# Projecting two column blocks with one 512-column product in a two-layer diffusion block

## The chip, the cores and the metric

The program runs on one core of a Trainium2 chip, in one launch. The metric is the device time of the whole program in microseconds, the median over the runs of a kernel. A profiled execution gives the trace; its times are counted from the first instruction of the span.

## What is computed

A two-layer backbone over 256 context and 512 latent tokens of width 1024. Each layer normalizes and modulates its input (`h`), projects it with one wide weight matrix, mixes tokens, gates, and projects back:

```
layer 0:  q, zf, zb, i, gate = split(h @ w_in, 5)      # each 2048 columns, 16 heads of 128
          o = bidirectional gated scan of (q, zf, zb, i), all 768 tokens
          y = rmsnorm(o) * norm_g * silu(gate);  x += gate_ada * (y @ w_out)
layer 1:  q, k, v, gate = split(h @ w_in, 4)           # each 2048 columns, 16 heads
          o = softmax(q1 k1) v - lam * softmax(q2 k2) v   (rotary q and k; 512 latent queries, 768 keys)
          y = rmsnorm(o) * g * silu(gate);  x += gate_ada * (y @ w_out)
final     rmsnorm(x)
```

So values (`i` in layer 0, `v` in layer 1) are wanted for all 768 tokens; the gate for all 768 in layer 0 and for the 512 latent ones in layer 1.

## The kernel before, in words

Every fp32 product of the projections is made of three products of split halves: a weight block is copied to `wH` (ACT, L269) and the remainder `wL = raw - wH` is made on DVE (L272); the input has `hH` and `hL`. A block of weights is a *unit* of 512 KB: it is loaded by SP's queue into one of four `raw` buffers (L261), split, and held in one of four `w` slots until TensorE (PE) has used it.

There are two kinds of projection. `proj_T` (L353) has the weights stationary and the tokens moving; it makes q, zf, zb of layer 0 and q, k of layer 1, one unit and one head at a time, with 256 and 512 moving columns. `proj_N` (L374) has 128 tokens stationary (`hH` or `hL`) and 256 weight columns moving; it makes the values and gates. One call is one token tile of 128: 8 blocks of the contraction times 3 products, 24 matmuls of 256 columns. `tok0` (layer 0) and `tok1` (layer 1) call it for a pair of heads: `tok0(p, "v")` and `tok0(p, "gate")` for six token tiles each, `tok1(p, "v1")` for six, `tok1(p, "sg")` for the four latent ones. There are eight pairs in each layer, so 8 x (6 + 6 + 6 + 4) x 24 = 4224 matmuls of this kind.

The order of all engines' instructions is written out by a planner, `Order`: processes (the scans or attention heads, the projections as one long process "fill", the loader, the two splits) yield priced operations, and the planner lists whichever can start first by its own prices; slots of buffers (`SLOTS`) are acquired and released on the way. `fill` takes the pieces in the order in which the end of the file lists them, and PE runs the scan's or the attention's short matmuls (L718, L740, L792, L807, L860, L889; L1403, L1404, L1433, L1442) between its steps. `out_proj` (L1066) projects back with 128 tokens of `y` stationary and 512 weight columns moving; the last `SLOTS["w"]` of its 16 blocks are taken together at the end, one token tile after the other (`rest`, L1100).

Two small jobs use `raw` directly, without a split: `ada_block` (L431; L445 on PE; four loads of 512 KB, half of the matmuls need the first two loads, half the last two) and `ada_gate`. Their units are put into the loader's list late: `piece` holds them back until at least `LATE` = 2 later units are listed (L308 to L322). In layer 0 the blocks `ada_block(1, b)` stand after zf of heads 10 to 13.

Of the kernel before, what the change touches and what calls it, by code (L numbers as in the profile page):

```python
# [35 lines left out]
RSQRT_SEED = 0x5F3759DF  # L36


SLOTS = {"bg": 2, "ps": 3, "pt": 1, "raw": 4, "raw0": 12, "w": 4, "y": 2, "q": 2, "FK": 2, "Q": 2, "t3": 3, "AD": 2,
         "A": 1, "S": 1, "KT": 2, "v": 2, "gate": 1, "hf": 2, "xgc": 2, "xnc": 2, "resc": 1, "jkc": 1, "hfc": 2,  # L40
         "Ks": 3, "S1": 3, "qL": 3, "rr": 2, "k": 1, "E": 2, "aT": 2, "v1": 2, "sg": 2}


# [157 lines left out]
def tile_kernel(ctx: ExitStack, tc: tile.TileContext, a: dict, out: bass.AP):  # L201
# [160 lines left out]
    def proj_N(acc, us, t, layer):  # L362

        n = KT * 3
        r = 1 if t < 2 else 0
        t0 = t - 2 + 2 * r
        sl = slice(t0 * P, (t0 + 1) * P)

        def step(kts):
            for kt in kts:  # L370
                un, k = us[kt // 4], kt % 4
                for j, (hh, W) in enumerate(((hH, un.H), (hH, un.L), (hL, un.H))):
                    i = 3 * kt + j
                    nc.tensor.matmul(acc, hh[r][:, kt, sl], W[:, k, :], start=(i == 0), stop=(i == n - 1))  # L374

        for kts in ((0, 1), (2, 3), (4, 5), (6, 7)):
            for kt in kts:
                yield wait(("h", layer, r, t0 // 2, kt))
            yield pe(6 * 0.109, lambda kts=kts: step(kts))


    start = ExitStack()
# [218 lines left out]
    def tok0(p, name, base):  # L601

        us = units_N(w0, base + p * 256)

        def evac(acc, ts):
            n = len(ts)
            pv = acc.rearrange("p (b c) -> p b c", c=256)[:, 0:n]
            dv = pairs[p][name][:, ts[0]:ts[0] + n]
            if name == "v":
                yield act(n * 256, lambda: nc.scalar.copy(out=dv, in_=pv))  # L610
            else:
                yield act(n * 256, lambda: nc.scalar.activation(out=dv, in_=pv, func=AF.Sigmoid))
                yield dve(n * 256, lambda: nc.vector.tensor_tensor(out=dv, in0=pv, in1=dv, op=ALU.mult))
            yield release("bg")
            if ts[0]:
                yield setev((name, p))

        def body():
            yield wait("scan")
            yield acquire(name)  # L620
            pairs[p][name] = env["sc"].tile([P, NT, 256], F32, name=name, tag=name, bufs=SLOTS[name])
            for ts in ((0, 1, 2, 3), (4, 5)):
                yield acquire("bg")
                acc = bg()
                for i, t in enumerate(ts):
                    yield from proj_N(acc[:, i * 256:i * 256 + 256], us, t, 0)
                yield spawn(evac(acc, ts), PR_EVAC)

        piece(us, body)

# [611 lines left out]
    def tok1(p, name, base):  # L1242
# [26 lines left out]

        piece(us, body)  # L1270

    def rope(acc, dst=None):

        at = env["ea"]
# [114 lines left out]
    def attention(n):  # L1389
# [99 lines left out]
            nc.vector.tensor_tensor(out=s["r"], in0=s["r"], in1=rs, op=ALU.mult)  # L1489

        def gated():
            s["y"] = env["at"].tile([P, 4, P], F32, name="y", tag="y1")
            for t in range(4):
                nc.vector.scalar_tensor_tensor(out=s["y"][:, t], in0=s["o"][:, t], scalar=s["r"][:, t:t + 1],
                                               in1=pair["sg"][:, t, cols], op0=ALU.mult, op1=ALU.mult)
# [4 lines left out]
                nc.tensor.transpose(s["pt"][:, t * P:(t + 1) * P], s["y"][:, t], ident)  # L1500

        def y_copy():
            yT = env["at"].tile([P, LAT], F32, name="yT", tag="y1")
# [148 lines left out]
    tok1(0, "v1", 2 * DI)  # L1652
    feat1_k(1)
    for n in range(NH):
        if n in (4, 5):
            piece(*ada_gate(1, n - 4, (0,)))
# [117 lines left out]
```

## Time and profile before

| | |
|---|---|
| runs | 1897.64, 1901.33, 1901.52 us; median 1901.33 us |
| the profiled execution | 1901.33 us, span of its instructions 1899.5 us |
| PE busy | 1858.8 us of the span (98%), 17910 matmuls |
| PE weight load / DVE / ACT busy | 1677.8 / 1250.5 / 932.6 us |
| mean DMA rate | 93 GB/s |

PE's busy time counts a matmul from its start until its result is out, and matmuls overlap; what a matmul costs in a stream is the distance from its start to the next one's start. The profiled execution is the median run, and its time is 1.8 us more than its span.

### The profile page before, as it was taken

Reading aid. Unit: us, or ns where it says so; the run is one execution under the profiler, and the core shown is the slowest. Engines: PE = TensorE matmul, PEld = TensorE weight load, DVE = VectorE, ACT = ScalarE, POOL = GpSimd, SP = SyncE. Lnnn points to the kernel's source line nnn. Section 1 sums busy time; section 2 is a strip of 40 time slices with the busy share of each in tenths; the row PEclk is TensorE's granted clock in tenths of the full one; section 3 lists DMA queues with packets and bytes.
Section 4 is the critical chain, followed back from the end, with each engine's and each line's share of the span. In section 5 each row is a group of like instructions: output and inputs, shape, how many; then the busy total and the mean of one; then the engine's idle time right before and its main releaser. Section 6 shows DMA issues by size and latency. Waiting matters only on the chain.

```text
span 1899.5 us, 41727 instructions
## 1 busy us (share of the span) xinstructions
PE 1858.8 (98%) x17910; PEld 1677.8 (88%) x17910; DVE 1250.5 (66%) x2492; ACT 932.6 (49%) x1716; POOL 29.9 (2%) x60
## 2 busy tenths in 40 slices
PE   5999999999999999999999899999999999999997
PEld 3898989999898998988988789999899999999986
DVE  4747657474664656657678776776667666766766
ACT  3434434343443434434455455665656565655753
POOL 0000000000000000000000100000000000000000
PEclk9999999999999999999999999999999999999999
DMA  9221121212313215131257751121322111121354
GB/s 312 60 68 52 44 75 44 64 36 73 101 33 116 72 54 159 50 109 46 66 168 259 227 163 45 33 68 51 110 86 73 42 60 51 51 73 67 104 201 172
DMA packets 166300, 177.59 MB, mean 93 GB/s; under 512 B 5857, under 2 KB 146066, under 8 KB 166114
## 3 DMA queue, kind: packets, MB, share of 16 engines
q1 hardware_dynamic: 160674, 156.08, 26.6%
q0 software_dynamic: 4864, 17.79, 2.7%
q8 instruction: 141, 2.31, 0.5%
q10 hardware_dynamic: 576, 1.05, 0.1%
q14 instruction: 45, 0.37, 0.1%
HBM read 161.52 MB, written 13.37 MB: 92 GB/s over the span
## 4 chain that ended last, share of the span: by engine, by line
PE 75%; issue 18%; DVE 3%; DMA 2%; ACT 1%; POOL 0%; SPq 0%; DVEq 0%; POOLq 0%; ACTq 0%
PE bg L353 21%; PE bg L374 15%; PE ps L353 7%; PE ps L374 7%; PE bg L1066 6%; PE ps L889 3%; PE ps L1442 3%; PE ps L740 2%; PE ps L860 2%; PE ps L1066 1%; PE bg L1403 1%; PE bg L1404 1%; PE pt L1433 1%; PE pt L840 1%; DVE wL L272 1%
## 5 line engine op out<-in xcount | busy, mean ns | idle before, releaser
L272 DVE TENSOR_TENSOR wL<-raw,wH 128x1024 fp32r<-128x1024 f32 x224 | 273.2, 1223 | 194.3 <-ACT wH L269 193.6
L269 ACT CAST wH<-raw 128x1024 fp32r<-128x1024 f32 x224 | 234.5, 1049 | 231.0 <-PE bg L353 88.4
L374 PE MATMUL bg<-wH,hH 128*128 128x256 f32 x768 | 226.8, 295 | 0.0
L374 PE MATMUL bg<-wH,hL 128*128 128x256 f32 x768 | 218.7, 285 | 0.0
L374 PE MATMUL bg<-wL,hH 128*128 128x256 f32 x768 | 218.2, 284 | 0.0
L353 PE MATMUL bg<-hH,wH 128*128 128x256 f32 x752 | 202.6, 350 | 1.4 <-ACT wH L269 1.2
L353 PE MATMUL bg<-hL,wH 128*128 128x256 f32 x752 | 194.0, 338 | 1.3 <-DVE hL L566 1.3
L353 PE MATMUL bg<-hH,wL 128*128 128x256 f32 x752 | 192.2, 337 | 0.0
L374 PE MATMUL ps<-wH,hH 128*128 128x256 f32 x640 | 186.4, 291 | 0.0
L374 PE MATMUL ps<-wL,hH 128*128 128x256 f32 x640 | 180.8, 282 | 0.0
L374 PE MATMUL ps<-wH,hL 128*128 128x256 f32 x640 | 180.7, 283 | 0.0
L1411 DVE TENSOR_REDUCE nm<-bg 128x1 f32<-128x768 f32 x128 | 118.9, 952 | 70.3 <-PE bg L1404 69.9
L353 PEld LDWEIGHTS bg<-hL,wH 128*128 128x128 f32 x752 | 141.3, 188 | 17.4 <-DVE hL L566 1.6
L353 PEld LDWEIGHTS bg<-hH,wL 128*128 128x128 f32 x752 | 141.2, 188 | 16.8 <-issue 0.2
L353 PEld LDWEIGHTS bg<-hH,wH 128*128 128x128 f32 x752 | 134.9, 189 | 19.7 <-issue 2.3
L374 PEld LDWEIGHTS bg<-wH,hH 128*128 128x128 f32 x768 | 146.9, 191 | 2.5
L353 PE MATMUL ps<-hH,wH 128*128 128x512 f32 (+1 forms) x400 | 147.2, 371 | 0.3 <-ACT hH L565 0.3
L374 PEld LDWEIGHTS bg<-wL,hH 128*128 128x128 f32 x768 | 147.0, 191 | 0.4
L1416 ACT ACTIVATE E<-bg,nm 128x768 f32<-128x768 f32 x128 | 115.6, 904 | 64.3 <-DVE nm L1411 62.7
L374 PEld LDWEIGHTS bg<-wH,hL 128*128 128x128 f32 x768 | 146.7, 191 | 0.3
L353 PE MATMUL ps<-hL,wH 128*128 128x512 f32 (+1 forms) x400 | 140.9, 355 | 0.1
L353 PE MATMUL ps<-hH,wL 128*128 128x512 f32 (+1 forms) x400 | 140.9, 355 | 0.0
(250 smaller groups left out, 3879.1 us busy)
## 6 DMA issues: line engine op xcount, KB each, us to landing
raw<-hg_w_in SPq DMA_DIRECT2D x80, 512.0 KB, 4.7
raw<-da_w_in SPq DMA_DIRECT2D x64, 512.0 KB, 4.1
raw<-w_ada SPq DMA_DIRECT2D x48, 512.0 KB, 4.3
raw<-hg_w_out SPq DMA_DIRECT2D x48, 512.0 KB, 4.4
raw<-da_w_out SPq DMA_DIRECT2D x32, 512.0 KB, 4.1
raw<-yT_d SPq DMA_DIRECT2D x15, 512.0 KB, 4.1
yT_d<-yT POOLq DMA_DIRECT2D x14, 384.0 KB, 4.2
yT_d<-yT POOLq DMA_DIRECT2D x14, 256.0 KB, 2.4
```

The costliest lines, as they stand in the source:

```text
L269: nc.scalar.copy(out=u.H, in_=u.raw)
L272: nc.vector.tensor_tensor(out=u.L, in0=u.raw, in1=u.H.bitcast(F32), op=ALU.subtract)
L353: nc.tensor.matmul(acc, W[:, kt, :], hh[r][:, kt, :], start=(i == 0), stop=(i == n - 1))
L374: nc.tensor.matmul(acc, hh[r][:, kt, sl], W[:, k, :], start=(i == 0), stop=(i == n - 1))
L740: nc.tensor.matmul(s["ps"][32 * b:32 * b + 32, (li + 1) % 2, c, :], s["C", li][:, o:o + 32], mv, start=True, stop=True, skip_group_check=T ...
L840: nc.tensor.transpose(s["pt"][:, i, d], st["K"][:, d, c * P:(c + 1) * P], ident)
L860: nc.tensor.matmul(s["sp"][:, i, d], s["KT", g][:, i, d], v[:, orders[d][k]], start=True, stop=True)
L889: nc.tensor.matmul(po[:, i], l, r, start=(k == 0), stop=(k == len(terms) - 1), skip_group_check=True)
L1066: nc.tensor.matmul(st["acc"][i][j], yy, W[:, 512 * j:512 * j + 512], start=(kt == 0 and k == 0), stop=(kt == NH - 1 and k == 2))
L1411: nc.vector.tensor_reduce(out=s["nm", qt][:, h:h + 1], in_=s["sc", qt, h][:, :, 0:384], axis=AX.XY, op=ALU.max, negate=True)
L1416: nc.scalar.activation(out=e, in_=s["sc", qt, h][:, :, 0:384], func=AF.Exp, bias=s["nm", qt][:, h:h + 1], accum_out=s["sums"][:, qt, h:h + 1])
L1442: nc.tensor.matmul(s["o"][:, qt], s["aT", qt][:, t], pair["v1"][:, t, cols], start=(t == 0), stop=(t == NT - 1), skip_group_check=True)
```

## The change

For seven of the eight pairs of each layer one piece takes the place of two: `both0` projects values and gate of a pair together, `both1` values and gate of layer 1. The moving operand is 512 columns, 256 of the values beside 256 of the gate, from units that hold 256 rows of the contraction and both column blocks; they are loaded with two DMAs each. A piece has four such units and needs all four for each token tile. The last pair of layer 0 and the first of layer 1 keep `tok0` and `tok1`. The value products of layer 1's two context tiles, which have no gate, stay 256 columns wide. The `w` slots become five, the `gate` slots two; `y` and `yT` of layer 1 share one buffer; the ada jobs move to other heads (`ada_gate` of layer 0 to after q of heads 4 and 6, `ada_block(1, b)` to after zf of heads 8, 10, 12, 14); the scratch for GpSimd's DMA descriptors is halved.

```diff
-SLOTS = {"bg": 2, "ps": 3, "pt": 1, "raw": 4, "raw0": 12, "w": 4, "y": 2, ...
-         "A": 1, "S": 1, "KT": 2, "v": 2, "gate": 1, "hf": 2, ...
+SLOTS = {"bg": 2, "ps": 3, "pt": 1, "raw": 4, "raw0": 12, "w": 5, "y": 2, ...
+         "A": 1, "S": 1, "KT": 2, "v": 2, "gate": 2, "hf": 2, ...
...
-        nc.sync.dma_start(out=u.raw, in_=u.src())
+        src = u.src()
+        if len(src.shape) < 4:
+            nc.sync.dma_start(out=u.raw, in_=src)
+        else:
+            for b in range(src.shape[2]):
+                nc.sync.dma_start(out=u.raw[:, :, b], in_=src[:, :, b])
...
+    def units_2(w, b, col):
+        return [Unit(lambda u=u: w[256 * u:256 * u + 256].rearrange("(k p) (b c) -> p k b c", p=P, c=DI)
+                     [:, :, b:b + 2, col:col + 256], [2, 2, 256], "w") for u in range(4)]
...
+    def proj_2(acc, us, t, layer, blocks=slice(0, 2)):
...
+        cost = 0.12 if blocks.stop == 1 else 0.23
+        def step(u):
+            for k in range(2):
+                kt, un = 2 * u + k, us[u]
+                for j, (hh, W) in enumerate(((hH, un.H), (hH, un.L), (hL, un.H))):
+                    i = 3 * kt + j
+                    nc.tensor.matmul(acc, hh[r][:, kt, sl], W[:, k, blocks].rearrange("p b c -> p (b c)"),
+                                     start=(i == 0), stop=(i == n - 1))
+        for u in range(4):
...
+            yield pe(6 * cost, lambda u=u: step(u))
...
+    def both0(p):
+        us = units_2(w0, 3, p * 256)
+        def evac(acc, t):
+            pv = acc.rearrange("p (t b c) -> p t b c", t=2, b=2)
+            v, g = (pairs[p][name][:, t:t + 2] for name in ("v", "gate"))
+            yield act(512, lambda: nc.scalar.copy(out=v, in_=pv[:, :, 0]))
+            yield act(512, lambda: nc.scalar.activation(out=g, in_=pv[:, :, 1], func=AF.Sigmoid))
+            yield dve(512, lambda: nc.vector.tensor_tensor(out=g, in0=pv[:, :, 1], in1=g, op=ALU.mult))
+            yield release("bg")
...
+            for t in range(0, NT, 2):
+                yield acquire("bg")
+                acc = bg()
+                for i in range(2):
+                    yield from proj_2(acc[:, i * 512:i * 512 + 512], us, t + i, 0)
+                yield spawn(evac(acc, t), PR_EVAC)
...
+    def both1(p):
+        us = units_2(w1, 2, p * 256)
...
+            if t < 2:
+                yield act(512, lambda: nc.scalar.copy(out=v[:, 0:2].rearrange("p t c -> p (t c)"), in_=acc))
+            else:
+                yield act(256, lambda: nc.scalar.copy(out=v[:, t], in_=acc[:, 0:256]))
+                yield act(256, lambda: nc.scalar.copy(out=g[:, t - 2], in_=acc[:, 256:512]))
+            yield release("ps")
...
-    tok0(0, "v", 3 * DI)
+    both0(0)
     for n in range(NH):
-        if n % 2 == 0 and n < NH - 2:
-            tok0(n // 2, "gate", 4 * DI)
         if n + 1 < NH:
             for i, (name, base) in enumerate(FEATS):
                 piece(*feat0(n + 1, unit_T(w0, base + (n + 1) * P), name))
-                if i == 0 and n in (7, 8):
-                    piece(*ada_gate(0, n - 7, (0, 1)))
-                if i == 1 and 9 <= n <= 12:
-                    piece(*ada_block(1, n - 9))
+                if i == 0 and n in (3, 5):
+                    piece(*ada_gate(0, (n - 3) // 2, (0, 1)))
+                if i == 1 and n in (7, 9, 11, 13):
+                    piece(*ada_block(1, (n - 7) // 2))
             if n % 2 and n < NH - 3:
-                tok0((n + 1) // 2, "v", 3 * DI)
+                both0((n + 1) // 2)
...
             feat1_k(n + 2)
             feat1_q(n + 2)
             if n % 2 == 0:
-                tok1((n + 2) // 2, "v1", 2 * DI)
-            else:
-                tok1((n + 1) // 2, "sg", 3 * DI)
+                both1((n + 2) // 2)
```

What the built programs show, at three places. On PE, the first token tile of the first pair of layer 0, from the last products of the head before; before:

```order
L353 MATMUL bg<-hL_82,wH 128x512
L353 MATMUL bg<-hH_81,wL 128x256
L353 MATMUL bg<-hH_80,wL 128x512
L374 MATMUL bg<-wH,hH_81 128x256
L374 MATMUL bg<-wL,hH_81 128x256
L374 MATMUL bg<-wH,hL_83 128x256
```

and now:

```order
L363 MATMUL bg<-hL_82,wH 128x512
L363 MATMUL bg<-hH_81,wL 128x256
L363 MATMUL bg<-hH_80,wL 128x512
L404 MATMUL bg<-wH,hH_81 128x512
L404 MATMUL bg<-wL,hH_81 128x512
L404 MATMUL bg<-wH,hL_83 128x512
```

One matmul stands where two stood. In the whole program 4224 of 256 columns become 1680 of 512 columns (L404), 336 of 256 columns for layer 1's context tiles (L404) and 528 that stay with `tok0` and `tok1` (L384); 17910 PE instruction records become 16230.

On PE, the first `ada_block(1, b)` of layer 0 (`raw` are its loaded weights, `sil` the stationary condition vectors); before, behind zf of head 10:

```order
L353 MATMUL bg_7158<-hH0_80,wL_6984 128x512
L740 MATMUL ps_7259<-Q_7141,C_7257 32x32 x24
L445 MATMUL ps_7308<-raw_7009,sil_100 32x128 x2
L445 MATMUL ps_7308<-raw_7051,sil_100 32x128 x2
...
L445 MATMUL ps_7308<-raw_7117,sil_100 32x128 x2
L445 MATMUL ps_7308<-raw_7209,sil_100 32x128 x2
```

and now, behind zf of head 8:

```order
L363 MATMUL bg_5246<-hH0_80,wL_4926 128x512
L476 MATMUL ps_5393<-raw_5134,sil_100 32x128 x2
L476 MATMUL ps_5393<-raw_5205,sil_100 32x128 x2
...
L800 MATMUL ps_5359<-Q_5229,C_5357 32x32 x24
L476 MATMUL ps_5393<-raw_5295,sil_100 32x128 x2
L363 MATMUL bg_5472<-hH1_81,wH_4968 128x256
...
L800 MATMUL ps_5476<-Q_5229,C_5444 32x32 x24
L363 MATMUL bg_5472<-hL0_82,wH_4968 128x512
L476 MATMUL ps_5393<-raw_5442,sil_100 32x128 x2
```

The fourth load's first product (`raw_5442`) now stands behind nine products of zb and two levels of the scan. On SP's queue the loads of that block, before and now, with what each waits for:

```order
L261 DMA raw_7009<-w_ada 128x4x256 [waits DMAHW5_49,DVE_49]
L261 DMA raw_7051<-w_ada 128x4x256 [waits DMAHW6_49,DVE_49]
L261 DMA raw_7117<-w_ada 128x4x256 [waits DMAHW7_49,DVE_49]
L261 DMA raw_7209<-w_ada 128x4x256 [waits DMAHW0_49,DVE_49]
```

```order
L263 DMA raw_5134<-w_ada 128x4x256 [waits DMAHW6_49,DMAHW5_49,DVE_49]
L263 DMA raw_5205<-w_ada 128x4x256 [waits DMAHW7_49,DMAHW0_49,DVE_49]
L263 DMA raw_5295<-w_ada 128x4x256 [waits DMAHW2_49,DMAHW1_49,DVE_49]
L263 DMA raw_5442<-w_ada 128x4x256 [waits DMAHW5_49,PE_49]
```

Before, all four loads wait for DVE, that is for a split that frees their buffer. Now the fourth waits for PE: its buffer is that of the first load, which the block's own first products read. The same stands at the blocks behind zf of heads 10 and 12; the one behind zf of head 14 has four loads that wait for DVE.

On PE, the finish of the last attention head in layer 1, from its last value products (`v` by `aT`) to the transposes of its result `y`; before (nine more rows of `out_proj` left out):

```order
L1066 MATMUL ps<-wH,yS_20245 128x512 x2
L1442 MATMUL ps<-v_19425,aT 128x128 x6
L1066 MATMUL bg<-wH,yKs 128x512 x2
...
L1066 MATMUL ps<-wL,hH_80 128x512 x2
L1066 MATMUL ps<-wH,hL_82 128x512 x2
L1066 MATMUL bg<-wH,yKs 128x512
L1500 MATMUL pt<-ident,y 128x128 x2
```

and now, all of them:

```order
L1547 MATMUL ps<-v_17852,aT 128x128 x6
L1126 MATMUL bg<-wL,yKs 128x512
L1126 MATMUL bg<-wH,yS_18693 128x512 x2
L1126 MATMUL bg<-wH,hH_80 128x512 x2
L1126 MATMUL bg<-wL,hH_80 128x512 x2
L1126 MATMUL bg<-wH,hL_82 128x512 x2
L1605 MATMUL pt<-ident,y 128x128 x4
```

Before, 25 products of `out_proj` stand between the two; now 9. The layer's last projections, which ran into the last head before, end while the head before it runs, and five blocks of `out_proj` instead of four are kept for the end.

At the program's start the order on ACT has one more split ahead of the first tokens: before, two `wH`, then `hH_80` and `hH_81` (the inputs of the first token tiles); now a third `wH` stands between `hH_80` and `hH_81`, since there is a fifth `w` slot.

## Rows read from the trace of the kernel before

**Rows 1.** The page: busy time, and PE's granted clock in 40 slices.

```profile
PE 1858.8 (98%) x17910; PEld 1677.8 (88%) x17910; DVE 1250.5 (66%) x2492; ACT 932.6 (49%) x1716; POOL 29.9 (2%) x60
...
PEclk9999999999999999999999999999999999999999
```

**Rows 2.** Windows: PE, PEld, DVE, ACT, POOL busy; clock; DMA share; GB/s.

```profile
0.00:60.00 60.00, 37.64 (x390) 27.36 (x390) 32.24 (x101) 22.90 (x39) 1.39 (x7) 1.00 0.84 266
...
240.00:352.00 112.00, 112.00 (x1428) 102.43 (x1427) 69.65 (x138) 46.16 (x88) 1.08 (x2) 1.00 0.18 55
...
1060.00:1110.00 50.00, 44.98 (x194) 35.55 (x193) 31.28 (x51) 20.93 (x28) 4.79 (x9) 0.97 0.72 218
...
1500.00:1600.00 100.00, 100.00 (x701) 94.55 (x700) 70.10 (x137) 60.36 (x118) 1.08 (x2) 1.00 0.18 56
...
1850.00:1900.00 50.00, 38.78 (x166) 30.72 (x164) 33.92 (x89) 19.49 (x29) 0.00 (x0) 0.94 0.47 164
```

**Rows 3.** Timeline of PE (start, us, engine, line), 256 columns moving, 96 products apart.

```profile
1433.24 0.28 PE L374 MATMUL ps<-wH,hH 128*128 128x256 f32 x1
...
1444.76 0.40 PE L353 MATMUL ps<-hH,wH 128*128 128x512 f32 x1
```

**Rows 4.** Timeline of PE, 512 columns: `out_proj`, 32 apart; `proj_T`, nine apart.

```profile
984.30 0.62 PE L1066 MATMUL bg<-wL,yF 128*128 128x512 f32 x2
...
991.73 0.63 PE L1066 MATMUL bg<-wH,yK 128*128 128x512 f32 x2
...
1448.95 0.39 PE L353 MATMUL ps<-hH,wH 128*128 128x512 f32 x1
...
1450.99 0.39 PE L353 MATMUL ps<-hH,wH 128*128 128x512 f32 x1
```

**Rows 5.** Groups by line and form on PE: values and gates.

```profile
L374 PE MATMUL bg<-wH,hH 128*128 128x256 f32 x768 | 226.8, 295 | 0.0
...
L374 PE MATMUL ps<-wH,hH 128*128 128x256 f32 x640 | 186.4, 291 | 0.0
```

**Rows 6.** Timeline of PE around the second `ada_block` of layer 1's parameters.

```profile
622.27 0.52 PE L353 MATMUL bg<-hL,wH 128*128 128x256 f32 x2
622.63 0.51 PE L353 MATMUL bg<-hH,wL 128*128 128x256 f32 x2
623.07 0.60 PE L740 MATMUL ps<-Q,C 128*32 128x32 f32 x46
...
623.52 1.93 PE L445 MATMUL ps<-raw,sil 128*32 128x128 f32 x62
625.38 0.61 PE L353 MATMUL bg<-hH,wH 128*128 128x256 f32 x2
```

**Rows 7.** The page, DMA issues: KB each and median us from issue to landing.

```profile
raw<-w_ada SPq DMA_DIRECT2D x48, 512.0 KB, 4.3
```

**Rows 8.** Timelines at the start: DVE, then PE's wait for it.

```profile
48.78 2.35 DVE L272 TENSOR_TENSOR wL<-raw,wH 128x1024 fp32r<-128x1024 f32 x2
...
51.79 0.49 PE L353 MATMUL bg<-hL,wH 128*128 128x512 f32 x1 [1.25 <-DVE hL L566]
```

**Rows 9.** Timeline of PE at the change of layers.

```profile
1080.79 0.89 PE L553 MATMUL ps<-ident,xn 128*128 128x128 f32 x4 [1.94 <-DVE hf L557]
...
1082.77 1.05 PE L1066 MATMUL bg<-wH,yK 128*128 128x512 f32 x2
1083.62 1.05 PE L1066 MATMUL bg<-wH,yF 128*128 128x512 f32 x2
```

**Rows 10.** Timeline of PE, the last head's last value products and transposes.

```profile
1828.53 1.50 PE L1442 MATMUL ps<-v,aT 128*128 128x128 f32 x12
...
1836.36 0.50 PE L1500 MATMUL pt<-ident,y 128*128 128x128 f32 x2 [0.54 <-DVE y L1494]
```

**Rows 11.** Waits: who waited for whom, us, times, longest.

```profile
DVE wL L272 <- ACT wH L269: 193.6, 103, 6.7
...
ACT wH L269 <- PE bg L353: 88.4, 19, 7.0
```

More of the change, by code (lines that the diff above doesn't have):

```diff
@@ L36 @@
 RSQRT_SEED = 0x5F3759DF
-SLOTS = {"bg": 2, "ps": 3, "pt": 1, "raw": 4, "raw0": 12, "w": 4, "y": 2, "q": 2, "FK": 2, "Q": 2, "t3": 3, "AD": 2,
-         "A": 1, "S": 1, "KT": 2, "v": 2, "gate": 1, "hf": 2, "xgc": 2, "xnc": 2, "resc": 1, "jkc": 1, "hfc": 2,
+SLOTS = {"bg": 2, "ps": 3, "pt": 1, "raw": 4, "raw0": 12, "w": 5, "y": 2, "q": 2, "FK": 2, "Q": 2, "t3": 3, "AD": 2,
+         "A": 1, "S": 1, "KT": 2, "v": 2, "gate": 2, "hf": 2, "xgc": 2, "xnc": 2, "resc": 1, "jkc": 1, "hfc": 2,
          "Ks": 3, "S1": 3, "qL": 3, "rr": 2, "k": 1, "E": 2, "aT": 2, "v1": 2, "sg": 2}
@@ L379, in proj_N @@
             yield pe(6 * 0.109, lambda kts=kts: step(kts))
+    def proj_2(acc, us, t, layer, blocks=slice(0, 2)):
+        n = KT * 3
+        r = 1 if t < 2 else 0
+        t0 = t - 2 + 2 * r
+        sl = slice(t0 * P, (t0 + 1) * P)
+        cost = 0.12 if blocks.stop == 1 else 0.23
[7 more added lines that the diff above has]
+        for u in range(4):
+            for kt in (2 * u, 2 * u + 1):
+                yield wait(("h", layer, r, t0 // 2, kt))
+            yield pe(6 * cost, lambda u=u: step(u))
     start = ExitStack()
@@ L627, in body @@
                 yield spawn(evac(acc, ts), PR_EVAC)
+        piece(us, body)
+    def both0(p):
[7 more added lines that the diff above has]
+            yield release("bg")
+            if t == NT - 2:
+                yield setev(("v", p))
+                yield setev(("gate", p))
+        def body():
+            yield wait("scan")
+            for name in ("v", "gate"):
+                yield acquire(name)
+                pairs[p][name] = env["sc"].tile([P, NT, 256], F32, name=name, tag=name, bufs=SLOTS[name])
+            for t in range(0, NT, 2):
[4 more added lines that the diff above has]
+                yield spawn(evac(acc, t), PR_EVAC)
         piece(us, body)
@@ L1270, in tok1, with tiles, evac, after @@
         piece(us, body)
+    def both1(p):
+        us = units_2(w1, 2, p * 256)
+        def tiles():
+            if "v1" not in apairs[p]:
+                apairs[p]["v1"] = env["at"].tile([P, NT, 256], F32, name="v1", tag="v1", bufs=SLOTS["v1"])
+                apairs[p]["sg"] = env["ea"].tile([P, NT - 2, 256], F32, name="sg", tag="sg", bufs=SLOTS["sg"])
+            return apairs[p]["v1"], apairs[p]["sg"]
+        def evac(acc, t):
+            yield wait("att")
+            v, g = tiles()
+            if t < 2:
[4 more added lines that the diff above has]
+            yield release("ps")
+            yield setev(("vg", p, t))
+        def after():
+            for t in (1, *range(2, NT)):
+                yield wait(("vg", p, t))
+            yield setev(("v1", p))
+            g = tiles()[1]
+            yield act(1024, lambda: nc.scalar.activation(out=g, in_=g, func=AF.Silu), extra=2.6)
+            yield setev(("sg", p))
+        def body():
+            yield acquire("v1")
+            yield acquire("sg")
+            for t in (*range(2, NT), 1):
+                yield acquire("ps")
+                acc = ps()
+                if t > 1:
+                    yield from proj_2(acc, us, t, 1)
+                else:
+                    for i in range(2):
+                        yield from proj_2(acc[:, 256 * i:256 * i + 256], us, i, 1, slice(0, 1))
+                yield spawn(evac(acc, t), PR_EVAC)
+            yield spawn(after(), PR_EVAC)
+        piece(us, body)
     def rope(acc, dst=None):
@@ L1491, in gated @@
         def gated():
-            s["y"] = env["at"].tile([P, 4, P], F32, name="y", tag="y1")
+            s["y"] = env["at"].tile([P, 4, P], F32, name="y", tag="y1", bufs=1)
             for t in range(4):
@@ L1502, in y_copy @@
         def y_copy():
-            yT = env["at"].tile([P, LAT], F32, name="yT", tag="y1")
+            yT = env["at"].tile([P, LAT], F32, name="yT", tag="y1", bufs=1)
             nc.scalar.activation(out=yT, in_=s["pt"], func=AF.Copy, scale=lc["gsub"])
@@ L1654, in tile_kernel @@
     for n in range(NH):
-        if n in (4, 5):
-            piece(*ada_gate(1, n - 4, (0,)))
+        if n in (4, 6):
+            piece(*ada_gate(1, (n - 4) // 2, (0,)))
         if n + 2 < NH:
@@ L1765 @@
     arrays.update(constants())
-    nc = _bacc.Bacc("TRN2", target_bir_lowering=False, num_devices=1, dynamic_dma_scratch_size=8192)
+    nc = _bacc.Bacc("TRN2", target_bir_lowering=False, num_devices=1, dynamic_dma_scratch_size=4096)
     aps = {n: nc.dram_tensor(n, v.shape, mybir.dt.from_np(v.dtype), kind="ExternalInput").ap()
```

## The prediction

> **What bounds the kernel now.** I read the page first. PE is busy for 1858.8 of 1899.5 us and its granted clock shows a 9 in all 40 slices [rows 1]. So PE is idle for 40.7 us, and no other engine comes near it: DVE is busy for 66% and ACT for 49%. The windows then say where that idle time lies [rows 2]: 22.4 us of it in the first 60 us, while the first weights and tokens come in, 5.0 us around the change of layers, 11.2 us in the last 50. In the two long stretches in which the values and gates are made, 240 to 352 us (layer 0) and 1500 to 1600 us (layer 1), PE is busy for the whole stretch at full clock (2.4 GHz), while DVE is busy for 69.65 of 112 us and 70.10 of 100, and ACT for 46.16 and 60.36. There only the price of PE's own instructions counts, and a new wait of PE is paid in full.
>
> A matmul's listed duration overlaps its neighbours, so I take distances between starts. 96 products of 256 columns take 1444.76 - 1433.24 = 11.52 us, or 120.0 ns each [rows 3]. 32 products of 512 columns in `out_proj` take 991.73 - 984.30 = 7.43 us, or 232.2 ns; nine in `proj_T` take 2.04 us, or 226.7 ns [rows 4]. So 512 columns cost a little less than twice 256.
>
> The sum is made against the profiled execution, 1901.33 us (its span and 1.8 us around it), which is also the median of the three runs.
>
> **Merged products (gain).** The groups of [rows 5] and their sisters hold 3 x 768 + 3 x 640 = 4224 products of 256 columns. The orders count 1680 pairs of them that become one of 512. A pair costs 2 x 120.0 = 240.0 ns. No row has a 512-column product with exactly these operands; the nearest is `out_proj`, which also has tokens stationary and split weights moving, 232.2 ns, and the fastest is `proj_T`, 226.7 ns. The gain per pair is 7.8 to 13.3 ns, or 13.1 to 22.3 us for 1680. I take 231 ns, close to the first, since its operands are the same in kind: 9.0 ns x 1680 = **-15.1 us**.
>
> The Trainium skill, page "TensorE: Matmul & The Clock Gate", section "Back-to-back issue gap", gives a stream's start-to-start time at full clock as N/2.4 + about 2.5 ns. By it, a merged pair saves one 2.5 ns, and the sum of this term, as an estimate from that page, would be -4.2 us. The rows do not bear that out: they show 120.0 and 227 to 232 ns where it has 109 and 216.
>
> **The moved ada blocks (loss).** These are small products of the condition vectors with `w_ada`, which need no split. Before, the four loads of an `ada_block` wait for splits on DVE and are in time: PE runs the block's 64 passes without a wait, from 623.52 to 625.38 [rows 6]. Now the fourth load of three blocks (behind zf of heads 8, 10 and 12) waits until PE has finished with the block's first buffer. From its issue to its landing such a load takes 4.3 us [rows 7]. PE's work in between, by the order: four more products of the block (0.06 us each, 1.86 / 32), two levels of the scan (623.07 to 623.52, 0.45 us each), ten products of zb, 256 and 512 columns in turn (0.36 us a pair, 622.27 to 622.63: 1.8 us): 0.24 + 0.9 + 1.8 = 2.9, some 3.0 us. The rest, 1.3 us, is a wait of PE, and behind it stands all of PE's stream, the next level of the scan too. Three times: **+3.9 us**. The ends are my choice around that median, since no row shows a disturbed load here: 3.2 us a load leaves 0.2 each, 0.6 in all; half as long again, 6.5 us, leaves 3.5 each, 11 in all.
>
> **The start (loss).** PE waits 1.25 us for `hL`, which DVE makes behind two `wL` of 2.35 us together [rows 8]. A third split now stands ahead of it on ACT and on DVE. One `wL` costs 1.2 us, and what it delays is that wait: between 0 (if DVE is free meanwhile) and 1.2; I take **+1.0 us**. The first pair now needs gate weights early, too. It begins 20 us later, so I price it at nothing; its cover is the last head-0 projection.
>
> **The last head (loss).** Before, the last value products end at 1828.53 + 1.50 = 1830.03 and the transposes of `y` begin at 1836.36: 6.3 us for squares, the reciprocal root and the gating on ACT and DVE [rows 10]. PE filled these with 25 products of `out_proj` and waited 0.54 us. Now 9 products stand there, 9 x 0.232 = 2.1 us, so the wait becomes 6.3 - 2.1 = 4.2, or 3.7 us more. The 16 products come later, where nothing needs cover, so this is lost. The chain may be shorter with fewer splits in between, or the scores before it may wait too: 0.5 to 8; I take **+3.8 us**.
>
> **At nothing.** Evacuations become 256 and 512 columns in other shapes, but ACT and DVE have 40 to 60 us to spare in 100 or so [rows 2]. Loads become two DMAs, 56 more issues on SP; at the DMA share of 0.18 in those windows the queue has room. The piece holds four of five `w` slots for some 33 us; the next unit's cast and `wL` must fit beside the one projection that is prefetched, 24 pairs of 0.35 us = 8.3 us, and they take 1.2 us each. If that cover is missing, see the slower rival. One buffer for `y` and `yT`: heads are some 40 us apart. The smaller scratch has no row; I take 0, bounds 0 to 2.
>
> **Sum:** -15.1 + 3.9 + 1.0 + 3.8 = -6.4, so about **1895 us**. With the small ends of the losses and the middle of the gain it is 1887; with the large ones 1906.
>
> **Rivals.** *(a) The gain without the losses.* The loads of the ada blocks come earlier than the order suggests, or the last chain is shorter. Then only the merging counts, -13 to -22 us: about 1885. For it: PE is 100% busy in the stretches at stake. Against it: the two waits follow from the order itself, not from a price.
>
> *(b) The gain is eaten.* The ada waits are at their large end, 11 instead of 3.9 us: 1895 + 7.1 = 1902. A clock loss can join it: behind the wait of 1.94 us at the change of layers, two pairs of 512-column products start 0.85 us apart, 425 ns a product [rows 9], the lower of the clock's two levels (1.2 GHz). Four such products behind each of three waits are 12 x (425 - 232) = 2.3 us more: 1904. For it: those idle times of 1.9 us are as short as a long ada wait. Against it: the median load, and a granted clock of 0.97 over the whole change of layers [rows 2].
>
> *(c) Slower: the pieces wait for splits.* A piece frees four slots within one token tile, and the splits of the next units queue on ACT behind evacuations. DVE's mean wait for a `wH` is 193.6 / 103 = 1.9 us, the longest 6.7 [rows 11]. If PE waits that long at the end of each of the 14 pieces, it is +26.6 us: 1895 + 26.6 = 1921.5. It decides from 6.4 / 14 = 0.46 us a piece. Against it: the 8.3 us of cover.
>
> *(d) The columns alone set the price.* Then 512 columns cost what 2 x 256 do, 240.0 ns, the gain is 0 and the losses remain: 1901.3 + 8.7 = 1910. For it: the two distances of [rows 3] and [rows 4] are nearly in the ratio of the columns. Against it: both rows of [rows 4] lie below 240. The page named above has nearly this rule, as it leaves 2.5 ns a pair.
>
> That the change does not do what it says is out: the orders count 1680 merged products and 16230 records on PE.
>
> **How the numbers follow.** My forecast has a chance of 0.50, with a range of its own from 1889 to 1900; rival (a) 0.22, (b) 0.17, (c) 0.06, (d) 0.05. The range goes from 1881, which takes in the middle of (a) and most of its gain, to 1905, which takes in (b). A measurement of this kernel tells 0.2% (3.8 us) from no change. Faster than 1897.5 are (a) and five sixths of the forecast: 0.22 + 0.42 = 0.64. Within 3.8 us are the rest of the forecast (0.08), (b) without its tail (0.14) and a little of (a) and (d): 0.25. Slower are (c), most of (d) and the tail of (b): 0.11.
>
> **What the profile after would show.** If the gain is right: starts of L404's 512-column products 230 to 232 ns apart, PE's busy time some 15 us less, in both long windows alike. If the ada step is right: waits of about 1.3 us on PE for the fourth load of three of the four blocks. If the end is right: a wait of some 4 us ahead of the last transposes of `y`, ended by DVE's `y`. Wrong would be: 237 ns or more a product, no wait at the ada blocks, or new idle time of PE behind each piece.

## The result, and the profile after

| | before | after |
|---|---|---|
| runs | 1897.64 to 1901.52 us | 1911.41 to 1917.63 us |
| median | 1901.30 us | 1913.24 us |
| ratio | | 1.0067 (95%: 1.0055 to 1.0079) |
| profiled execution's span | 1899.5 us | 1910.6 us |

The change made the kernel 12 us slower. The forecast was 1895 us, and the range ended at 1905. The page of the changed kernel, its lines on busy time and on the clock (to be read beside [rows 1]):

```profile
PE 1852.3 (97%) x16230; PEld 1586.8 (83%) x16230; DVE 1249.6 (65%) x2499; ACT 933.8 (49%) x1758; POOL 30.2 (2%) x60
...
PEclk9999999999999999999999899999999999999999
```

PE's busy time fell by 6.5 us, not by 15, and its idle time rose from 40.7 to 1910.6 - 1852.3 = 58.3 us, by 17.6. Most of it stands in PE's waits after (who waited for whom: us in all, times, longest):

```profile
PE ps L476 <- DMA raw<-w_ada: 13.7, 5, 9.9
PE pt L1605 <- DVE y L1599: 10.5, 7, 6.6
PE ps L584 <- DVE hf L588: 10.0, 3, 8.1
...
PE ps L800 <- DVE AD L804: 1.1, 2, 0.7
...
PE ps L1126 <- ACT hH L1613: 0.8, 1, 0.8
PE ps L920 <- ACT KT L904: 0.6, 1, 0.6
```

and before:

```profile
PE ps L445 <- DMA raw<-w_ada: 12.3, 3, 10.7
PE ps L553 <- DVE hf L557: 4.9, 2, 2.9
...
PE pt L1500 <- DVE y L1494: 0.5, 1, 0.5
...
PE ps L740 <- DVE AD L744: 0.3, 1, 0.3
```

Two waits grew by 15.1 us together: for `y` at the transposes of a head's result, 0.5 to 10.5, and for `hf`, the input of layer 1, 4.9 to 10.0. The waits for `w_ada` grew by 1.4 in all and by 2.2 behind the start. The merged products themselves are cheap, as the timeline of PE at the first piece shows:

```profile
72.96 0.40 PE L404 MATMUL bg<-wH,hH 128*128 128x512 f32 x1
...
79.78 0.39 PE L404 MATMUL bg<-wH,hH 128*128 128x512 f32 x1
```

The second row is the 30th product after the first: 6.82 us / 30 = 227.3 ns, against 240.0 for the two that it replaces [rows 3]. (Over layer 0's undisturbed products, those between two of their own kind, the distances lie between 220 and 250 ns, 229 on average, in the same trace, whose starts come in steps of 10 ns.) So the gain was there, and something took back more than it gave. The windows around the change of layers and at the end add a second loss, the granted clock (the column after the five engines; before [rows 2]):

```profile
1060.00:1110.00 50.00, 41.88 (x180) 33.52 (x179) 29.01 (x49) 19.26 (x26) 3.94 (x8) 0.90 0.68 204
1110.00:1200.00 90.00, 88.64 (x586) 81.91 (x585) 68.97 (x120) 50.90 (x88) 0.00 (x0) 0.98 0.25 74
...
1850.00:1911.00 61.00, 50.06 (x208) 40.09 (x208) 42.58 (x105) 24.59 (x37) 0.00 (x0) 0.92 0.40 137
```

0.90 around the change of layers where it was 0.97, and 0.92 in the end part where it was 0.94. Behind the longest wait of the end part, products of 512 columns run at the lower level of the clock, as they did behind the shorter waits of before [rows 9]; the timeline of PE there:

```profile
1850.47 1.16 PE L1605 MATMUL pt<-ident,y 128*128 128x128 f32 x4 [6.64 <-DVE y L1599]
1852.40 1.22 PE L1126 MATMUL ps<-wH,hH 128*128 128x512 f32 x2 [0.78 <-ACT hH L1613]
1853.42 1.05 PE L1126 MATMUL ps<-wL,hH 128*128 128x512 f32 x2
1854.28 1.05 PE L1126 MATMUL ps<-wH,hL 128*128 128x512 f32 x2
```

The last two start 0.86 us apart, a pair of products in each row, where 0.46 is usual.

**The wait for `hf`.** It ends the chain DMA, ACT, DVE, PE. One row of each, from their timelines after:

```profile
1036.73 14.22 SPq L263 DMA_DIRECT2D raw<-hg_w_out  x4
...
1060.97 0.38 SPq L263 DMA_DIRECT2D raw<-yT_d  x1
```

```profile
1074.11 1.04 ACT L274 CAST yF<-raw 128x1024 fp32r<-128x1024 f32 x1 [8.32 <-DMA raw<-yT_d]
```

```profile
1075.19 1.23 DVE L277 TENSOR_TENSOR yK<-raw,yF 128x1024 fp32r<-128x1024 f32 x1 [6.03 <-ACT yF L274]
```

```profile
1079.51 0.69 PE L584 MATMUL ps<-ident,xn 128*128 128x128 f32 x2 [8.12 <-DVE hf L588]
```

DVE runs its operations in the order listed. It stands 6.03 us at the split of a block of `y` whose load was issued at 1060.97 and was there at about 1074, 13 us later, and `hf` is queued behind that split. Two groups of loads ahead of it on SP's queue, four loads of `hg_w_out` were drawn out over 14.22 us, as they waited for buffers. This gave the first theory: **the kept blocks.** With five `w` slots, `out_proj` keeps five blocks for the end of each pair of token tiles (L1160 after), uses them for one token tile after the other and frees them only with the second, and the loads stand still meanwhile. The second: **the late heads.** The piece puts a pair's gates ahead of the next head's k and q. Each odd head then starts later against the projections, and the last head outlives them. A third: **the long steps.** The planner hands out six 512-column products at a time (1.37 us instead of 0.72), and the heads' short products wait longer.

### The profile page after: what moved, and what is told of

The parts are those of the page before. It is cut to its first block, busy times and chain, and to the rows that moved or that the text cites. A ratio compares the mean times of both kernels' runs of the same rounds, so it can differ in the third digit from the quotient of the medians.

```text
span 1910.6 us, 38544 instructions
## 1 busy us (share of the span) xinstructions
PE 1852.3 (97%) x16230; PEld 1586.8 (83%) x16230; DVE 1249.6 (65%) x2499; ACT 933.8 (49%) x1758; POOL 30.2 (2%) x60
## 4 chain that ended last, share of the span: by engine, by line
PE 71%; issue 20%; DVE 4%; DMA 3%; ACT 2%; POOL 0%; SPq 0%; DVEq 0%; POOLq 0%; ACTq 0%
PE bg L363 20%; PE bg L404 13%; PE bg L1126 6%; PE ps L404 6%; PE ps L363 5%; PE ps L949 3%; PE ps L1547 2%; PE ps L800 2%; PE ps L920 2%; PE bg L384 2%; PE ps L1126 2%; PE bg L1508 1%; DVE wL L277 1%; PE pt L1538 1%; PE bg L1509 1%
## 5 line engine op out<-in xcount | busy, mean ns | idle before, releaser
L404 PE MATMUL bg<-wH,hH 128*128 128x512 f32 x336 | 138.0, 411 | 0.0
L404 PE MATMUL bg<-wL,hH 128*128 128x512 f32 x336 | 131.7, 392 | 0.0
L404 PE MATMUL bg<-wH,hL 128*128 128x512 f32 x336 | 131.6, 392 | 0.0
L404 PE MATMUL ps<-wH,hH 128*128 128x512 f32 (+1 forms) x336 | 123.9, 369 | 0.0
L789 ACT COPY C<-K 128x768 f32<-128x768 f32 x80 | 74.4, 930 | 98.7 <-DVE K L814 83.7
L404 PE MATMUL ps<-wH,hL 128*128 128x512 f32 (+1 forms) x336 | 120.0, 357 | 0.0
L404 PE MATMUL ps<-wL,hH 128*128 128x512 f32 (+1 forms) x336 | 119.1, 355 | 0.0
L1543 ACT COPY aT<-pt 128x512 f32<-128x512 f32 (+1 forms) x128 | 61.3, 479 | 100.6 <-PE pt L1538 100.3
L1547 PEld LDWEIGHTS ps<-v,aT 128*128 128x128 f32 x768 | 95.2, 191 | 4.0
```

The source lines that it names most:

```text
L404: nc.tensor.matmul(acc, hh[r][:, kt, sl], W[:, k, blocks].rearrange("p b c -> p (b c)"), start=(i == 0), stop=(i == n - 1))
L789: nc.scalar.copy(out=C.rearrange("p (n d s) -> p n d s", d=2, s=z), in_=view(st["K"], 0, [[2 * z, TOK // (2 * z)], [TOK + z, 2], [1, z]]))
L1543: nc.scalar.copy(out=s["aT", qt][:, lo:hi].rearrange("p a b -> p (a b)"), in_=s["pt"][:, 0:(hi - lo) * P])
L1547: nc.tensor.matmul(s["o"][:, qt], s["aT", qt][:, t], pair["v1"][:, t, cols], start=(t == 0), stop=(t == NT - 1), skip_group_check=True)
```

## Experiments

**1. Four kept blocks, five slots.**

```diff
-            if kt >= NH - SLOTS["w"]:
+            if kt >= NH - 4:
```

> The changed kernel with four instead of five blocks kept for the end of each out_proj; five w slots stay. Theory of the kept blocks (the fifth w slot makes out_proj keep five blocks, so loads stand still while these are used, and the waits at the change of layers, 9.8 us for hf, and at the last head, 6.6 us for y, follow from that): the wait for hf falls to about 5 us as before, the time falls by 4 to 8 us, to 1905 to 1909. Theory of the late heads (the one long piece puts the gates ahead of the next head's k and q, so the last head ends late and outlives the projections): the wait for y stays at 5 to 8 us, the time changes by less than 3 us.

Measured: 1900.34 us, ratio to before 0.9999 (0.9988 to 1.0010): 12.9 us less than the changed kernel, more than either theory gave. Its waits of PE:

```profile
PE pt L1605 <- DVE y L1599: 10.3, 7, 5.8
PE ps L584 <- DVE hf L588: 3.7, 2, 3.5
```

The wait for `hf` fell (10.0 to 3.7, below the 4.9 of before), the wait for `y` stayed. So the kept blocks explain the change of layers, and not the last head. The four loads that took 14.22 us now take 7.67, on SP's timeline; the kernel before, then this one:

```profile
1042.01 6.80 SPq L261 DMA_DIRECT2D raw<-hg_w_out  x4
```

```profile
1036.94 7.67 SPq L263 DMA_DIRECT2D raw<-hg_w_out  x4
```

What holds them up in the changed kernel stands on ACT, in the cast of a block of `y`; the kernel before, the changed one, and this one:

```profile
1044.76 1.05 ACT L269 CAST yF<-raw 128x1024 fp32r<-128x1024 f32 x1 [1.24 <-PE bg L1066]
```

```profile
1047.84 1.05 ACT L274 CAST yF<-raw 128x1024 fp32r<-128x1024 f32 x1 [6.80 <-PE bg L1126]
```

```profile
1041.95 1.05 ACT L274 CAST yF<-raw 128x1024 fp32r<-128x1024 f32 x1 [1.23 <-PE bg L1126]
```

Blocks 8 to 11 of `out_proj` (of 0 to 15) read one of the two buffers for `y`, which is given back when block 11 has been used for the second token tile. With blocks 12 to 15 kept, that comes ahead of the end part. With five kept, block 11 is one of them, and the next `y` waits until PE is through with all five for the first token tile and with block 11 for the second. Its cast stands ahead of the next weights' casts in ACT's order, so the buffers that the loads want stay taken: SP waits 7.9 us for the split of this `y`. That it is this buffer, more than the slots of the weights, is read from the code and these rows, not tried by itself.

The granted clock from 1060 to 1110 us is 0.97 again. The profiled execution took 1905.61 us, the longest of this kernel's ten runs; its span of 1903.8 us is 6.8 less than that of the changed kernel.

**2. The fifth slot alone, in the kernel before.**

```diff
-"raw0": 12, "w": 4,
+"raw0": 12, "w": 5,
...
-name="y", tag="y1")
+name="y", tag="y1", bufs=1)
...
-name="yT", tag="y1")
+name="yT", tag="y1", bufs=1)
...
-dynamic_dma_scratch_size=8192
+dynamic_dma_scratch_size=4096
```

> The kernel before with the fifth w slot alone (and the smaller buffers that make room for it: one buffer for y and yT, the halved scratch); all projections as before, 256 columns. Theory of the kept blocks: 5 to 10 us slower than before, 1906 to 1911, with waits for hf of 8 to 10 us and for y of 3 us or more. Theory of the late heads: within 2 us of before, 1899 to 1903, a wait for y below 1 us.

Measured: 1908.33 us, ratio 1.0042 (1.0028 to 1.0056), 7.6 us slower than before without one merged product. PE's wait for `hf`, and the draw-out of the four loads on SP's timeline:

```profile
PE ps L553 <- DVE hf L557: 9.6, 3, 7.8
```

```profile
1044.79 14.22 SPq L261 DMA_DIRECT2D raw<-hg_w_out  x4
```

PE has no row of waiting for `y` at all. (In ACT's order the cast of `y` waits 6.80 us for PE here too.) The theory of the kept blocks holds for the change of layers, and its guess about the last head was wrong.

**3. The same with four kept blocks** (experiment 2 with the edit of experiment 1).

> Against e2_w5 (1908.3 us): the kernel before with the fifth w slot (and the smaller buffers) and four blocks kept for the end of out_proj; no merged products. Theory of the kept blocks: the wait for hf falls from 9.6 us to about 5, the time by 5 to 8 us, to that of the kernel before within 2 us (1899 to 1903). Rival (the fifth slot costs by itself, in the order of loads and splits): 1905 or more.

Measured: 1902.05 us, ratio 1.0004 (0.9995 to 1.0013); the wait for `hf` is 4.2 us in all. The fifth slot, the smaller buffers and the halved scratch cost nothing that can be measured; keeping five blocks does, 6.3 us here. (The two kernels of experiment 6 also differ by this alone: 8.0 us.)

**4. The last pair of layer 1 separate** (in the changed kernel: `tok1` for its values, then k and q of head 15, then `tok1` for its gates).

```diff
-            if n % 2 == 0:
+            if n % 2 == 0 and n < NH - 4:
                 both1((n + 2) // 2)
+            elif n == NH - 4:
+                tok1(NH // 2 - 1, "v1", 2 * DI)
+            elif n == NH - 3:
+                tok1(NH // 2 - 1, "sg", 3 * DI)
```

> The changed kernel with the last pair of layer 1 separate again: its values before k and q of head 15, its gates after them. Theory of the late heads: head 15 starts some 10 us earlier against the end of the projections, the wait for y at the last head falls from 6.6 us to 0 to 3, the time by 3 to 7 us, to 1906 to 1910, although 96 pairs of products (about 1 us) are no longer merged. Theory of the kept blocks: the wait for y stays near 6 us, and the time is 0 to 2 us longer, 1913 to 1915.

Measured: 1910.00 us, ratio 1.0045 (1.0030 to 1.0060), 3.2 us less than the changed kernel, though the two intervals overlap; and the wait at the last head stayed, 6.35 us. The time went the way of the theory and its reason did not. The timeline of PE says why:

```profile
1763.33 0.40 PE L363 MATMUL ps<-hH,wL 128*128 128x512 f32 x1
...
1783.34 0.34 PE L1509 MATMUL bg<-Ks,qL 128*128 128x384 f32 x1
1789.07 0.42 PE L1508 MATMUL bg<-Ks,S 128*128 128x384 f32 x1
```

q of head 15 is complete at 1763.33, but its first score starts only at 1789.07, as head 14's last one came at 1783.34. Head 14 was late; by the order, head 13 was late ahead of it, as its k and q still stood behind a piece. One pair was not enough to try the theory.

**5. Two pairs separate, and four kept blocks** (heads 12 to 15; experiment 1 and, for both pairs, the edit of experiment 4).

> Against e1_rest4 (1900.3 us): four blocks kept, and the last two pairs of layer 1 (heads 12 to 15) separate, their gates after the next head's k and q. In its order 24 products of out_proj stand between the last value products and the transposes of y, where e1_rest4 has 4. Theory of the late heads: the wait for y at the last head (5.8 us in e1_rest4) falls below 1 us, the time by 3 to 6 us, to 1894 to 1897, less about 2 us that 192 pairs no longer merge. Rival (the chain of the last head itself is longer in this program, whatever the order of the pieces): a wait of 4 us or more stays, the time is that of e1_rest4 or up to 2 us more.

Measured: 1895.82 us, ratio 0.9974 (0.9964 to 0.9984), 4.5 us under experiment 1, although 192 pairs of products are no longer merged. Timelines of PE, the last product of q of head 15 and its first score, and later the last value products and the transposes of `y`; the kernel after first, then this one:

```profile
1782.30 0.40 PE L363 MATMUL ps<-hH,wL 128*128 128x512 f32 x1
...
1796.34 0.42 PE L1508 MATMUL bg<-Ks,S 128*128 128x384 f32 x1
```

```profile
1756.80 0.40 PE L363 MATMUL ps<-hH,wL 128*128 128x512 f32 x1
...
1769.65 0.34 PE L1508 MATMUL bg<-Ks,S 128*128 128x384 f32 x1
...
1776.58 0.28 PE L384 MATMUL ps<-wH,hL 128*128 128x256 f32 x1
...
1824.60 1.50 PE L1547 MATMUL ps<-v,aT 128*128 128x128 f32 x12
...
1832.23 1.01 PE L1605 MATMUL pt<-ident,y 128*128 128x128 f32 x4 [0.59 <-DVE y L1599]
```

After the change, q of head 15 was the last projection of all, and the head's first score came 14 us behind it. Here that score comes 6.9 us ahead of the last product of the gates (L384), as before, where head 15's first score also stood ahead of the last gate products, by 4.3 us:

```profile
1780.41 0.42 PE L1403 MATMUL bg<-Ks,S 128*128 128x384 f32 x1
...
1784.66 0.28 PE L374 MATMUL ps<-wH,hL 128*128 128x256 f32 x1
```

The last wait for `y` falls from 5.8 to 0.59 us. Nine products cover the last head's chain in the changed kernel, from the end of its last value products to the transposes of `y`, and that chain is longer there:

```profile
1840.10 1.66 PE L1547 MATMUL ps<-v,aT 128*128 128x128 f32 x12
```

```profile
1846.45 1.23 DVE L277 TENSOR_TENSOR wL<-raw,wH 128x1024 fp32r<-128x1024 f32 x1 [1.18 <-ACT wH L274]
```

It takes 8.7 us (1841.76 to 1850.47), and in its midst DVE waits 1.18 us for a cast and then makes a split of 1.23 us. Here the chain takes 6.1 us (1826.10 to 1832.23), as before (6.3 [rows 10]). The theory of the late heads holds, for the last two pairs together.

**6. Steps of three products**, alone in the changed kernel and, second, with four kept blocks.

```diff
-            yield pe(6 * cost, lambda u=u: step(u))
+        for kt in range(KT):
+            yield wait(("h", layer, r, t0 // 2, kt))
+            yield pe(3 * cost, lambda kt=kt: step(kt))
```

> The changed kernel with the new piece handed to the planner in steps of three products (0.69 us) instead of six (1.37 us); the arithmetic is the same. Theory of the long steps (a step of six 512-column products keeps PE from the scans' and heads' short products, whose chains then come late): the waits for DVE's AD, for ACT's KT and for y inside the layers (together 5 us) fall below 2 us, the time by 4 to 8 us. Theories of the kept blocks and of the late heads: the two large waits (hf 9.8, last y 6.6) stay within 2 us of where they are, the time changes by less than 3 us.

> Against e1_rest4 (1900.3 us): four blocks kept, and the new piece in steps of three products. Theory of the long steps: 3 to 5 us less, 1895 to 1897, as the steps alone took 3.8 us off the changed kernel; the two effects add. If they act on the same waits: no more than 1 us less than e1_rest4.

Measured: 1909.45 us alone (3.8 less than the changed kernel, ratio to before 1.0042, 1.0027 to 1.0057), and 1901.46 with four kept blocks (1.0001, 0.9992 to 1.0011), 1.1 us more than without the short steps. The waits for AD and KT stay (1.9 us together, before 1.7), and what the first saved is in part at the two large waits (8.2 for `hf`, 8.3 for `y`). Beside four kept blocks the short steps gain nothing, so the long steps are not the cause of the loss.

**7. The planner's price**, with four kept blocks.

```diff
-        cost = 0.12 if blocks.stop == 1 else 0.23
+        cost = 0.109 if blocks.stop == 1 else 0.21
```

> Against e1_rest4 (1900.3 us): four blocks kept, and the planner's price of the new products lowered from 0.23 to 0.21 us (measured: 0.227 to 0.229), 0.12 to 0.109 for the narrow ones, so that PE falls behind its plan in these pieces as it did in the kernel before (0.109 against 0.120). Theory of the tight price (with a right price the planner puts the heads' products where their operands are only just, or not quite, ready): the waits for y inside the layer (together 4.5 us in e1_rest4) fall below 2 us, the time by 2 to 5 us. Rival (the order shifts, the waits turn up elsewhere): within 2 us of e1_rest4.

Measured: 1900.34 us, ratio 0.9996 (0.9987 to 1.0005), by chance the time of experiment 1 to the hundredth. The waits for `y` inside the layer fell as the theory had it, from 4.5 to 1.6 us (10.3 to 7.4 with the last head's), and the time did not. PE's waits for `w_ada` rose from 13.9 to 14.6, and 0.8 for `gRow` is new. The rival had it: an order moved by a price trades waits.

**8. Ada loads listed earlier**, with four kept blocks.

```diff
-    LATE = 2
+    LATE = 1
```

> Against e1_rest4 (1900.3 us): four blocks kept, and the ada loads listed one unit earlier (LATE 1 instead of 2). In its order no ada load waits for PE any more. Theory of the ada loads (PE waits for the fourth load, whose buffer the block itself frees): the waits of PE for w_ada after the first 60 us (2.4 us in e1_rest4) fall below 0.3 us, the time by 2 to 3 us, to 1897 to 1898. Rival (the loads then push back the next splits): those waits go, others of the same size come, within 1 us of e1_rest4.

Measured: 1912.44 us, ratio 1.0065 (1.0041 to 1.0089), 12.1 us slower than experiment 1. PE's waits:

```profile
PE ps L476 <- DMA raw<-w_ada: 11.6, 3, 9.9
...
PE ps L867 <- DVE Q L809: 10.3, 4, 2.8
```

The waits for `w_ada` behind the start are gone (11.6 is the start), and four new ones of up to 2.8 us stand at the scan, one a block, for `Q`. On DVE, at the first of them, that operation is queued behind a split that waits for its cast:

```profile
518.78 1.22 DVE L277 TENSOR_TENSOR wL<-raw,wH 128x1024 fp32r<-128x1024 f32 x1 [1.37 <-ACT wH L274]
519.92 0.95 DVE L814 TENSOR_TENSOR K<-K,T 128x768 f32<-128x768 f32 x1
520.79 0.95 DVE L809 TENSOR_TENSOR Q<-Q,T 128x768 f32<-128x768 f32 x1
```

The rival had the mechanism, and its size (within 1 us) was wrong: waits of 2.4 us went, and waits of 10.3 us came. That the ada loads now take buffers ahead of the piece's units, whose splits then come late, is read from these rows and the order, not tried by itself.

**9. Ada blocks at other heads**, with four kept blocks and two pairs separate.

```diff
-                if i == 1 and n in (7, 9, 11, 13):
-                    piece(*ada_block(1, (n - 7) // 2))
+                if i == 1 and n in (6, 8, 10, 12):
+                    piece(*ada_block(1, (n - 6) // 2))
```

Behind an odd `n` a new piece lists its four units ahead of the ada loads; behind an even one it doesn't.

> Against e8_two_pairs (1895.8 us): the four ada blocks of layer 1's parameters moved to after zf of heads 7, 9, 11 and 13, where no new piece of four units is listed between the block and its loads. In its order all of these loads wait for DVE, none for PE. Theory of the ada loads: the waits of PE for w_ada after the first 60 us (about 2 us) fall below 0.3 us, the time by 1 to 3 us, to 1893 to 1895. Rival, as in e12_late (loads that come earlier push back the next splits, DVE's Q comes late and PE waits for that at the scan's products, 2.5 to 3 us a block): the time rises by 5 to 12 us.

Measured: 1891.49 us, ratio 0.9945 (0.9933 to 0.9958), 4.3 us under experiment 5. The waits for `w_ada` are those of the start alone; experiment 5, then this kernel:

```profile
PE ps L476 <- DMA raw<-w_ada: 12.2, 6, 9.9
```

```profile
PE ps L476 <- DMA raw<-w_ada: 11.7, 3, 10.1
```

In experiment 5's trace the three waits behind the start were only 0.7 us together, and the two profiled spans lie 2.2 us apart (1891.7 and 1889.5). So the direction is that of the theory, but most of the 4.3 us is not tied to these waits. This is the version that beats both kernels: 9.8 us faster than before.

**10. The merging alone undone**, in experiment 5: the same order, each merged product issued as two.

```diff
-                    nc.tensor.matmul(acc, hh[r][:, kt, sl], W[:, k, blocks].rearrange("p b c -> p (b c)"),
-                                     start=(i == 0), stop=(i == n - 1))
+                    for b in range(blocks.stop):
+                        nc.tensor.matmul(acc[:, 256 * b:256 * b + 256], hh[r][:, kt, sl], W[:, k, b],
+                                         start=(i == 0 and b == 0), stop=(i == n - 1), skip_group_check=True)
```

> Against e8_two_pairs (1895.8 us): the same kernel and order, but each of its 1488 merged products is issued as two of 256 columns. Theory (a merged pair saves PE 8.5 ns in layer 1 and 11 ns in layer 0, and PE's stream sets the end): 13 to 17 us slower, 1909 to 1913. Rival (the merging is worth little on the path, because what PE saves comes back as waits for the heads and scans): at most 6 us slower, below 1902, with fewer waits of PE.

Measured: 1910.30 us, ratio 1.0047 (1.0034 to 1.0060), 14.5 us slower than experiment 5. Its page, beside that of experiment 5:

```profile
PE 1862.9 (98%) x17910; PEld 1678.3 (88%) x17910; DVE 1250.4 (66%) x2499; ACT 931.9 (49%) x1750; POOL 30.1 (2%) x60
```

```profile
PE 1847.0 (98%) x16422; PEld 1593.8 (84%) x16422; DVE 1249.5 (66%) x2499; ACT 931.7 (49%) x1750; POOL 30.1 (2%) x60
```

PE's busy time differs by 15.9 us. Its idle time is the same, 44.8 us (1907.7 - 1862.9) and 44.7 (1891.7 - 1847.0), although single waits shifted: those for `w_ada` are 2.8 us longer, those for `hf` and `y` 2.2 shorter. From the medians, 14.5 us / 1488 = 9.7 ns a merged pair; at an uncertainty of some 3 us that is 8 to 12 ns. The merging is worth what PE's stream says, and all of it reaches the end.

Beside the kernel before, this one has as many products and is 9.0 us slower, with the two large waits of the changed kernel already cut. So what else the change did costs that much, before any gain: PE is busy for 4.1 us more and idle for 4.1 us more.

## Why the prediction was wrong

- **The gain was right.** Forecast 9.0 ns a pair and -15.1 us; experiment 10 measures 9.7 ns, which for the 1680 pairs of the change is 16.3 us. What failed are the losses: 1913.2 - (1901.3 - 16.3) = 28.2 us, where the sum had 8.7 and its large ends together 20.2. Rival (d) gave a time nearest to the result, 1910, by a reason that is refuted: a merged product takes 227 to 229 ns, not 240. A right number for the wrong reason is no support. The Trainium skill ("TensorE: Matmul & The Clock Gate", section "Back-to-back issue gap") gives the N/2.4 + 2.5 ns of the prediction, but calls it the isolated gap of a single product and sets it apart from a stream with a weight load for each product, which this kernel has; the prediction left that out. By the formula, as an estimate, a pair would save 2.5 ns; the runs show 9.7.
- **The step that failed stands under "At nothing".** That part went through evacuations, loads, slots for the next splits, `y`'s buffer and the scratch, and held the fifth `w` slot for harmless. It did not ask where else its number is used. `out_proj` takes the number of slots as the number of blocks it keeps; the part ahead of the prediction even says so, and the sum priced it at nothing there. The fifth block holds back a buffer of `y` (6.80 us instead of 1.24 at the cast) and with it the loads, 14.22 us for four of them, and at the change of layers a split on DVE then waits for a late load, with `hf` behind it. Experiments 2 and 3 price this at 6.3 to 7.6 us without a merged product, experiment 1 at 12.9 us in the changed kernel. The trace of before showed the place: two waits for `hf`, 4.9 us together, of which I read only the clock behind the second [rows 9].
- **The last head: right place, undersized.** Forecast a wait of 4.2 us (+3.7); measured 6.64 us, 0.78 behind it for `hH`, and the clock. The nine covering products were right. The chain that they cover was taken from before, 6.3 us, and took 8.7 (experiment 5). The prediction gave a reason for a shorter chain, fewer splits in between, and none for a longer one, though its large end (8 us) took the size in. What left so few products for cover was q of head 15 as the last projection (experiment 5); the fifth kept block, which the part ahead of the prediction names beside it, was not it (experiment 1). By experiment 5 the late heads cost 4.5 us and, for the 192 pairs given up, 192 x 9.7 ns = 1.9: 6.4 us in all, an estimate. Shorter waits for `y` inside the layer (the 10.5 less the 6.64: 3.9 us) were not forecast, and no run here ties them to one cause.
- **The ada blocks: right in kind, oversized as waits.** Forecast 3 waits, +3.9 us; measured 2 waits, 2.2 us behind the start. Experiment 9, which takes such waits away, gains 4.3 us, but only 0.7 us of waits were there to take.
- **The start: nothing.** Forecast +1.0; PE waits 1.2 us for `hL`, as before [rows 8]. The lower end held.
- **Rival (c)**, waits of PE for splits behind each piece, didn't come: PE's waits for `wH` are 1.2 us in all, as many as before, at the start.
- **Left open.** Of the 28.2 us the experiments price 12.9 (kept blocks, forecast 0), 6.4 (late heads, forecast 3.8) and 4.3 (ada blocks, forecast 3.9); 4.6 us are tied to nothing, and each of these numbers is uncertain by some 3 us. PE's busy time fell by 6.5 us, not 16. Some of the rest is the clock: by the windows, 50 x 0.07 + 90 x 0.02 (0.98 from 1110 to 1200 us, 1.00 before) + about 2 us at the end is some 7 us at most, and a part of that lies in idle time. Another 4.1 us of PE's busy time came with the rest of the change (experiment 10). And experiment 1 moved the median by 12.9 us but the profiled span by 6.8. Its profiled execution was its longest, 5.3 us above the median, so the trace shows less than the medians do; which waits differ in its other runs cannot be seen.

## What to carry to other kernels

When a change enlarges a buffer, look up every place in the code that reads the size: a number that a second rule uses (blocks kept, units listed ahead) moves waits in stages that the change never meant to touch. A wait that the profile shows before the change, however short, is a place to look first: there nothing covers a further delay, and here 4.9 us of waits for `hf` became 10.0. And an operation merged with another one comes when the earlier of the two is needed, so what stood between them comes later: here the next head's k and q. In mid-stream other products covered most of that; where the stream ends, nothing did.

## What was not expected of the hardware

In this kernel earlier loads were worse than late ones: listing the ada loads one unit earlier took away waits of 2.4 us and made others of 10.3 us (experiment 8), by the rows through ACT's and DVE's order. And loads of one size took very different times from issue to landing: the median of `yT_d` loads is 4.2 us after the change, yet the one at 1060.97 took about 13 us. POOL issued a store and six loads of its own between 1058.97 and 1062.60 us in that trace, and from 1060 to 1110 us the DMA was busy for 0.68 of the time while moving 204 GB/s; that these delayed it is likely, but no run took them away. The kernel before has the like: a store of POOL at 1062.90, a `yT_d` load issued at 1064.50, and ACT's cast that waits for it until 1074.19, 9.7 us. So a slow load at this place is not new with the change.
